# Two of the four block sums of a quad by accumulating DMAs, with the operands in another order

## The chip, the core and the metric

The kernel runs on one core of a Trainium2 chip. The metric is the device time of one execution in microseconds (us); the time before is the median of three runs. Engines are named as in the profile: PE is TensorE (matmuls), PEld its weight load, DVE VectorE, ACT ScalarE, POOL GpSimd, and SP SyncE, which here only issues DMAs. Each engine works through its own queue of instructions in order and waits on semaphores for the others.

## The reference

One decoder block on 256 tokens of width 2048, all in float32: a mixer (gated linear attention beside a short gated convolution, merged by two sigmoid gates) and a SwiGLU network, each behind an RMSNorm and with a residual, and a last RMSNorm.

```python
h = h + hybrid_mixer(rmsnorm(h, mix_norm_w[l]), w_in[l], ...)
h = h + swiglu(rmsnorm(h, ffn_norm_w[l]), w_gate_up[l], w_down[l])
return rmsnorm(h, final_norm_w)

proj = jnp.einsum('bsd,de->bse', h, w_in)          # 2048 -> 16400 columns
(q, k, v, g_out, gk_low, gate_b, gate_c, xc, merge_a, merge_b) = jnp.split(proj, SPLIT_IDX, axis=-1)
y_a = (o * silu(g_out)); y_b = gate_b * causal_depthwise_conv(gate_c * xc, conv_w)
merged = sigmoid(merge_a) * y_a + sigmoid(merge_b) * y_b
out = jnp.einsum('bse,ed->bsd', merged, w_out)

gu = jnp.einsum('bsd,df->bsf', h, w_gate_up)       # 2048 -> 2 x 5632
gate, up = jnp.split(gu, [FFN_HIDDEN], axis=-1)
out = jnp.einsum('bsf,fd->bsd', silu(gate) * up, w_down)
```

Nearly all of the work is in the four weight matrices: `w_in`, `w_out`, `w_gate_up` and `w_down`.

## The kernel before

**Pieces.** Every weight matrix is cut into pieces of 128 partitions x 1024 float32 (512 KB), which the host lays out so that one DMA brings one piece. `stream_list` is the order in which the pieces are used, from the first k, q, v columns through the gates and the output projection to the hidden layer and the down projection.

**Split in two.** A float32 product is made of three matmuls in the fp32r type (`mm3`, lines 347 to 349): each operand is split into a high part and a rest. For a weight piece, ACT casts the raw tile to `hi` (line 238) and DVE subtracts to get `lo` (line 243). There are five raw tiles (`wraw`), six `hi` and five `lo`. `load_piece` issues a piece's DMA (line 232 or 295, on SP) and its cast, and `finish_low` the subtraction one piece later; `take` keeps this at most five pieces ahead of PE (`LOOK`).

**Plain pieces.** Most groups of 512 columns are worked through piece by piece (`eights`, `down`): two rows of blocks times two halves of the tokens, twelve matmuls for a piece.

**Quads with seven products.** Twelve pairs of groups, four in the gates (`gc0`/`xc0` to `gc3`/`xc3`) and eight of the hidden layer's (`fg`/`fu` 0, 3 to 7, 9 and 10), are computed with seven block products instead of eight, a form of Strassen's method (`sevens`). For each of four quads q of such a pair there are four blocks of weights, two of the first key and two of the second. The seven products of a quad are called 11, t1, t3, t2, t4, 21 and 22, six matmuls each. 11, 21 and 22 take a loaded block as it is. t1 to t4 take sums of blocks, made by `sum_of`: tile `y` holds block 11, tile `x` the second key's first block; t1 is y + x, written to a raw tile (line 259); then x grows in place by a third block (t3), by y (t2) and by a fourth block (t4), each time by a DVE addition (line 265). The third and the fourth block are loaded into raw tiles first. Between two of these additions x must have been cast and subtracted, so `sum_of` calls `finish_low` ahead of the next.

**The order.** `seven_list` names the products of a pair: for each quad 11, t1, t3, t2, t4, and at the end the 21 and 22. `mixed` deals the plain pieces that run beside a pair out among them, one behind each sum (with more than 16 of them a second round begins with the 21 and 22). `FIRST` places the first hidden pair by hand among the plain pieces of the output projection. What the code records is put on each engine's queue by a scheduling layer that may move instructions, except those that are pinned (`pin`).

**Round it.** POOL issues the copies and loads of the convolution (`conv`, lines 886 to 894) and three loads of h (line 1007). The gates' results are merged on DVE (lines 907 and 908, pinned) and transposed on PE (`transpose_block`, line 595). A group's PSUM bank comes free when DVE or ACT has taken its result, for the down projection the addition on line 1098; the plain groups have three banks in turn (`lent`).

Of the kernel before, what the change touches and what calls it, by code (L numbers as in the profile page):

```python
# [8 lines left out]
F32 = mybir.dt.float32  # L9
# [3 lines left out]
ALU = mybir.AluOpType  # L13
AX = mybir.AxisListType

P = 128
# [3 lines left out]
KC = D // P  # L20
# [60 lines left out]

FIRST = {0: (6, 6, 8, 10, 12), 1: (14, 14, 16, 18, 20), 2: (22, 22, 23, 24, 26), 3: (28, 28, 29, 30, 31)}
FIRST_END = (31, 32)
SEVENS = ((3, 16), (4, 15), (5, 16), (6, 15), (7, 16), (9, 15), (10, 15))
PLAIN = (1, 2, (0, (0, 1, 2)), (1, (3, 4, 5)), 8, (2, (6, 7, 8)))

# [8 lines left out]
    return first + [p for g in out[3:] for p in g]  # L97


def seven_list(pair):  # L100

    out = [(what, q) for q in range(4) for what in ("11", "t1", "t3", "t2", "t4")]
    twos = (("21", 0), ("21", 1), ("22", 0), ("21", 2), ("22", 1), ("21", 3), ("22", 2), ("22", 3))
    return [(pair, e) for e in out + list(twos)]


def mixed(pair, eights, early=False):

    if pair is None:
        return eights  # L110
    sevens = seven_list(pair)
    sums = ("t1", "t3", "t2", "t4")
    gaps = [0] * len(sevens)
    rest = len(eights)
    while rest > 0:
        for some in (sums + ("11",) if early else sums, ("21", "22")):
            for n, (_, e) in enumerate(sevens):
                if e[0] in some and rest > 0:
                    gaps[n] += 1
                    rest -= 1  # L120
    out, put = [], 0
    for e, n in zip(sevens, gaps):
        out += [e] + eights[put:put + n]
        put += n
    return out


def gates_list():
    return [e for pair, keys in GATES
            for e in mixed(pair, [(key, k) for key in keys for k in range(0, KC, 2)], keys[0] == "gb2")]  # L130


def block_of(key):
# [9 lines left out]
def hidden_list():  # L143

    plain = []
    for what in PLAIN:
        if isinstance(what, tuple):
            part, fs = what
            plain += [e for n in range(len(DOWN[part])) for f in fs for e in down_of(part, n, f)]
        else:  # L150
            plain += [(f"{name}{what}", k) for name in ("fg", "fu") for k in range(0, KC, 2)]
    plain = [(f"wo{n}", k) for n in range(1, 4) for k in range(0, KC, 2)] + plain

    before = {(what, q): FIRST[q][n] for q in range(4) for n, what in enumerate(("11", "t1", "t3", "t2", "t4"))}
    pair = seven_list(("fg0", "fu0"))
    for n, (_, e) in enumerate(pair[20:]):
        before[e] = FIRST_END[0] + n * (FIRST_END[1] - FIRST_END[0]) // 7
    out, put = [], 0
    for key, e in pair:
        out += plain[put:before[e]] + [(key, e)]  # L160
        put = before[e]
# [23 lines left out]
def block_kernel(ctx, tc, x, xt, cols_in, gkw_in, gku_in, gnw, conv_w, finw, w_in, w_out, w_gu, w_dn, out):  # L185
    nc = tc.nc
    pin = tc.keep_in_program_order
    mats = {"w_in": w_in, "w_out": w_out, "w_gu": w_gu, "w_dn": w_dn}

    const = ctx.enter_context(tc.tile_pool(name="const", bufs=1))  # L190
    wraw = ctx.enter_context(tc.tile_pool(name="wraw", bufs=5))
    whi = ctx.enter_context(tc.tile_pool(name="whi", bufs=6))
    wlo = ctx.enter_context(tc.tile_pool(name="wlo", bufs=5))
    aT = ctx.enter_context(tc.tile_pool(name="aT", bufs=1))
# [26 lines left out]
        rows[mat] = rows.get(mat, 0) + 1  # L221
    ready = {}
    hooks = {}
    count = {"loaded": 0, "used": 0, "tick": 0}
    pending = []
    held = {}
    halfway = []

    def fetch(key, k0, pool=wraw, tag="raw"):
        mat, j, n, w = index[(key, k0)]  # L230
        raw = pool.tile([P, n, w], F32, tag=tag, name=tag, bufs={"x": 2, "y": 1}.get(tag))
        nc.sync.dma_start(raw, mats[mat][j].rearrange("p (k c) -> p k c", c=w))
        return raw

    def high(raw, piece, a=0, b=None):
        hi, n = piece[0], piece[2]
        ks = slice(a, b or n)
        nc.scalar.copy(hi[:, ks, :], raw[:, ks, :])  # L238

    def low(raw, piece, a=0, b=None):  # L240
        hi, lo, n = piece
# [3 lines left out]
    def sum_of(pair, what, q):  # L245

        one, two = pair
        if what == "21":
            return fetch(one, 4 * q + 2)
        if what == "22":  # L250
            return fetch(two, 4 * q + 2)
        if what == "11":
            held["y"] = fetch(one, 4 * q, held["pool"], "y")
            return held["y"]
        y = held["y"]
        if what == "t1":
            held["x"] = fetch(two, 4 * q, held["pool"], "x")
            raw = wraw.tile([P, 2, 512], F32, tag="raw", name="raw")
            nc.vector.tensor_tensor(out=raw, in0=y, in1=held["x"], op=ALU.add)  # L259
# [5 lines left out]
        nc.vector.tensor_tensor(out=x, in0=x, in1=other, op=ALU.add)  # L265
        return x

    def load_piece():


        i = count["loaded"]
        count["loaded"] += 1
        if i < len(stream):
            key, k0 = stream[i]
            if isinstance(k0, tuple):
                n, w = 2, 512
                raw = sum_of(key, *k0)
                step = n
            else:
                mat, j, n, w = index[(key, k0)]  # L280
                raw = wraw.tile([P, n, w], F32, tag="raw", name="raw")

                step = n // 2 if i < 2 else n
            piece = [whi.tile([P, n, w], F32R, tag="hi", name="hi"), None, n]
            if isinstance(k0, tuple):
                high(raw, piece)
                halfway.append((raw, piece, key, k0))
            else:
                if i < 2:
                    piece[1] = wlo.tile([P, n, w], F32R, tag="lo", name="lo")  # L290
                for a in range(0, n, step):
                    b = a + step
                    if (i, a) in hooks:
                        hooks.pop((i, a))()
                    nc.sync.dma_start(
                        raw[:, a:b, :], mats[mat][j, :, a * w:b * w].rearrange("p (k c) -> p k c", c=w))
# [944 lines left out]
```

## Time and profile before

| | |
|---|---|
| three runs | 1506.49, 1505.09, 1506.01 us; median 1506.01 |
| the profiled execution | 1504.81 us, of which the span from the first to the last instruction is 1503.1 |
| granted TensorE clock, mean | 0.999 |
| HBM read | 351.03 MB, 235 GB/s over the span |
| DMA queues' share of 16 engines' span | SP's 70.8%, POOL's 2.2%, ACT's 0.3% |
| casts of x on ACT (line 238) | 144, waiting 207.1 us in total for DVE's sums |
| POOL's longest waits | 353.5 us in four, for the convolution's input |

The stages by time: the attention part to about 203 us, the gates to about 700, output projection and the first hidden pair to about 850, hidden layer and down projection to about 1475, and then the last norm and the stores.

How to read the rows: a group shows line, engine, operation, out<-in with shapes, the count, busy time, mean nanoseconds of one, and the idle time ahead of them with what ended it. A row of the timeline shows the start, the duration, engine and line. A row of the stages shows, behind its two bounds, the length and then each engine's busy time, TensorE's clock, the DMA engines' busy share and the rate. A row of the DMA issues ends with the size of one and the median time from issue to landing.

### The profile page before, as it was taken

The numbers are of one execution on the slowest core, as the hardware profiler recorded it, in microseconds if no ns is written. First come the engines' busy times: TensorE is split into PE (matmuls) and PEld (weight loads), VectorE is DVE, ScalarE is ACT, GpSimd is POOL, SyncE is SP. The second block draws the span as 40 slices with busy tenths as digits, with TensorE's granted clock in tenths as the row PEclk, the third lists the DMA queues.
The fourth block names the chain that finished last, engine by engine and source line by source line (L and its number), as shares of the span: only waits on it lengthen the run. The fifth ranks groups of instructions, "written<-read, shape, count | busy, mean of one in ns | idle before, by whom it ended". The sixth has DMA issues, their size and how long they took to land.

```text
span 1503.1 us, 19370 instructions
## 1 busy us (share of the span) xinstructions
PE 1489.7 (99%) x7064; PEld 1244.8 (83%) x7064; DVE 1277.8 (85%) x1283; ACT 864.1 (57%) x977; POOL 38.0 (3%) x60
## 2 busy tenths in 40 slices
PE   9999999999999999999999999999999999999997
PEld 8989988888887888888888888888888788888887
DVE  6785868979979878966689999999999999999975
ACT  7773546655655655654566755655565556565553
POOL 0030000000000000000000000000000000000000
PEclk9999999999999999999999999999999999999999
DMA  9656557876876878787677777776877788787782
GB/s 349 201 172 174 177 166 251 288 225 234 285 259 232 297 237 257 249 258 215 209 221 219 238 253 251 250 253 218 275 242 239 259 255 277 242 264 234 231 297 90
DMA packets 100128, 358.58 MB, mean 239 GB/s; under 512 B 11492, under 2 KB 11620, under 8 KB 99904
## 3 DMA queue, kind: packets, MB, share of 16 engines
q1 hardware_dynamic: 96656, 346.73, 70.8%
q0 software_dynamic: 2800, 8.89, 2.2%
q10 hardware_dynamic: 576, 1.72, 0.3%
q8 instruction: 55, 0.90, 0.2%
q14 instruction: 41, 0.34, 0.1%
HBM read 351.03 MB, written 2.10 MB: 235 GB/s over the span
## 4 chain that ended last, share of the span: by engine, by line
PE 53%; DVE 1%; issue 0%; ACT 0%; DVEq 0%; ACTq 0%
PE fg L347 8%; PE fg L349 8%; PE fg L348 8%; PE dn L347 5%; PE dn L349 5%; PE dn L348 5%; PE wo L347 2%; PE wo L348 2%; PE wo L349 2%; PE fu L349 1%; PE fu L347 1%; PE fu L348 1%; PE trb L595 1%; PE mb L349 0%; PE mb L348 0%
## 5 line engine op out<-in xcount | busy, mean ns | idle before, releaser
L243 DVE TENSOR_TENSOR lo<-raw,hi 128x1024 fp32r<-128x1024 f32 (+1 forms) x506 | 612.0, 1217 | 110.9 <-ACT hi L238 27.9
L238 ACT CAST hi<-raw 128x1024 fp32r<-128x1024 f32 (+1 forms) x506 | 523.9, 1047 | 269.9 <-PE gb L349 27.7
L238 ACT CAST hi<-x 128x1024 fp32r<-128x1024 f32 x144 | 151.7, 1053 | 267.4 <-DVE x L265 207.1
L243 DVE TENSOR_TENSOR lo<-x,hi 128x1024 fp32r<-128x1024 f32 x144 | 176.1, 1223 | 37.5 <-ACT hi L238 26.6
L347 PE MATMUL dn<-lo,acth 128*128 128x512 f32 (+1 forms) x368 | 140.7, 382 | 1.7 <-DVE h L1098 0.9
L349 PE MATMUL dn<-hi,acth 128*128 128x512 f32 (+1 forms) x368 | 139.9, 380 | 0.0
L348 PE MATMUL dn<-hi,actl 128*128 128x512 f32 (+1 forms) x368 | 139.9, 380 | 0.0
L265 DVE TENSOR_TENSOR x<-x,raw 128x1024 f32<-128x1024 f32 x96 | 117.0, 1218 | 12.0 <-DMA raw<-in_w_in_dram 7.7
L347 PE MATMUL fg<-lo,hh 128*128 128x512 f32 x288 | 112.4, 390 | 0.0
L349 PE MATMUL fg<-hi,hh 128*128 128x512 f32 x288 | 112.2, 390 | 0.0
L348 PE MATMUL fg<-hi,hl 128*128 128x512 f32 x288 | 112.2, 389 | 0.0
L347 PE MATMUL fg<-lo,sh 128*128 128x512 f32 x256 | 101.0, 395 | 0.0
L348 PE MATMUL fg<-hi,sl 128*128 128x512 f32 x256 | 99.9, 390 | 0.0
L349 PE MATMUL fg<-hi,sh 128*128 128x512 f32 x256 | 99.8, 390 | 0.0
L347 PEld LDWEIGHTS dn<-lo,acth 128*128 128x128 f32 x368 | 69.2, 188 | 15.8 <-DVE h L1098 1.8
L349 PEld LDWEIGHTS dn<-hi,acth 128*128 128x128 f32 x368 | 69.2, 188 | 13.3
L348 PEld LDWEIGHTS dn<-hi,actl 128*128 128x128 f32 x368 | 69.2, 188 | 12.9
L347 PEld LDWEIGHTS fg<-lo,hh 128*128 128x128 f32 x288 | 54.1, 188 | 11.8 <-DVE lo L243 0.5
L349 PEld LDWEIGHTS fg<-hi,hh 128*128 128x128 f32 x288 | 54.1, 188 | 11.3
L348 PEld LDWEIGHTS fg<-hi,hl 128*128 128x128 f32 x288 | 54.1, 188 | 11.0
L243 DVE TENSOR_TENSOR lo<-y,hi 128x1024 fp32r<-128x1024 f32 x48 | 58.5, 1218 | 4.8 <-ACT hi L238 2.1
L259 DVE TENSOR_TENSOR raw<-y,x 128x1024 f32<-128x1024 f32 x48 | 58.5, 1219 | 4.2 <-DMA y<-in_w_in_dram 3.3
(247 smaller groups left out, 3070.1 us busy)
## 6 DMA issues: line engine op xcount, KB each, us to landing
raw<-in_w_in_dram SPq DMA_DIRECT2D x254, 512.0 KB, 4.5
raw<-in_w_gu_dram SPq DMA_DIRECT2D x176, 512.0 KB, 4.4
raw<-in_w_dn_dram SPq DMA_DIRECT2D x88, 512.0 KB, 4.5
x<-in_w_gu_dram SPq DMA_DIRECT2D x32, 512.0 KB, 4.8
y<-in_w_gu_dram SPq DMA_DIRECT2D x32, 512.0 KB, 3.9
raw<-in_w_out_dram SPq DMA_DIRECT2D x32, 512.0 KB, 4.3
y<-in_w_in_dram SPq DMA_DIRECT2D x16, 512.0 KB, 4.4
x<-in_w_in_dram SPq DMA_DIRECT2D x16, 512.0 KB, 4.8
```

The lines of the kernel that those rows point to most:

```text
L238: nc.scalar.copy(hi[:, ks, :], raw[:, ks, :])
L243: nc.vector.tensor_tensor(out=lo[:, ks, :], in0=raw[:, ks, :], in1=hi[:, ks, :].bitcast(F32), op=ALU.subtract)
L259: nc.vector.tensor_tensor(out=raw, in0=y, in1=held["x"], op=ALU.add)
L265: nc.vector.tensor_tensor(out=x, in0=x, in1=other, op=ALU.add)
L347: nc.tensor.matmul(ps, lhsT=sh, rhs=ml, start=first, stop=False, skip_group_check=onto)
L348: nc.tensor.matmul(ps, lhsT=sl, rhs=mh, start=False, stop=False, skip_group_check=onto)
L349: nc.tensor.matmul(ps, lhsT=sh, rhs=mh, start=False, stop=last, skip_group_check=onto)
L595: nc.tensor.transpose(out=ps[:, j, :], in_=src[:, j * P:(j + 1) * P], identity=ident)
```

## The change

In a quad t3 and t4 are no longer summed by DVE. When t1's sum is recorded, POOL issues a DMA that adds the third block from HBM onto `x` in place (`add_piece`, accumulating); when t2's rest has been recorded, another one adds the fourth block. DVE keeps t1 and t2. The casts of t3 and t4 on ACT are pinned. The raw tiles of the third and fourth block fall away. There are now two `y` tiles: one is the old one, the other takes the place of the fifth raw tile, and the plain raw tiles have four in turn once the first pair has begun.

The order of the products changes: 11, t1, then t4 of the quad before, t3, t2; the last t4 stands among the products at the end (21 four times, 22 twice, t4, 22 twice). `mixed` now deals at least 16 plain pieces, or three quarters of them, to the quads: of four in a quad, three go behind t1 and one behind t3; the rest are spread over the nine at the end. `FIRST` is now a first position and, for each quad, the numbers of plain pieces behind t1, t4, t3 and t2. The `early` case is gone.

```diff
-FIRST = {0: (6, 6, 8, 10, 12), 1: (14, 14, 16, 18, 20), 2: (22, 22, 23, 24, 26), 3: (28, 28, 29, 30, 31)}
-FIRST_END = (31, 32)
+FIRST = (6, ((0, 3, 1, 4), (0, 3, 1, 4), (0, 3, 1, 2), (0, 3, 1, 0)), (1, 0, 0, 1, 0, 0, 0, 0, 0))
...
+def seven_list(pair, gaps):
+    out = []
+    for q in range(4):
+        ahead, fourth, third, second = gaps[q]
+        out += [("11", q, 0), ("t1", q, ahead)]
+        if q:
+            out += [("t4", q - 1, fourth)]
+        else:
+            out[-1] = ("t1", q, ahead + fourth)
+        out += [("t3", q, third), ("t2", q, second)]
+    twos = [("21", 0), ("21", 1), ("21", 2), ("21", 3), ("22", 0), ("22", 1), ("t4", 3), ("22", 2), ("22", 3)]
+    out += [(what, q, n) for (what, q), n in zip(twos, gaps[4])]
+    return [(pair, (what, q), n) for what, q, n in out]
...
+    n = len(eights)
+    quads = max(min(n, 16), n * 3 // 4)
+    gaps = []
+    for q in range(4):
+        c = (quads + 3 - q) // 4
+        places = [0] * 4
+        for i in (0, 0, 0, 2, 3, 1, 0, 2, 3, 1)[:c]:
+            places[i] += 1
+        gaps.append(places)
+    rest = n - quads
+    gaps.append([(i + 1) * rest // 9 - i * rest // 9 for i in range(9)])
...
-    wraw = ctx.enter_context(tc.tile_pool(name="wraw", bufs=5))
+    wraw = ctx.enter_context(tc.tile_pool(name="wraw", bufs=1))
...
+    def raw_tile(n, w):
+        count["raw"] += 1
+        return wraw.tile([P, n, w], F32, tag=f"raw{count['raw'] % count['raws']}", name="raw")
+
+    def first_tile():
+        count["y"] += 1
+        count["raws"] = 4
+        if count["y"] % 2:
+            return wraw.tile([P, 2, 512], F32, tag="raw4", name="y")
+        return held["pool"].tile([P, 2, 512], F32, tag="y", name="y")
...
         if what == "t1":
-            held["x"] = fetch(two, 4 * q, held["pool"], "x")
-            raw = wraw.tile([P, 2, 512], F32, tag="raw", name="raw")
-            nc.vector.tensor_tensor(out=raw, in0=y, in1=held["x"], op=ALU.add)
+            x = held["x", q] = held["pool"].tile([P, 2, 512], F32, tag="x", name="x", bufs=2)
+            fetch(two, 4 * q, x)
+            raw = raw_tile(2, 512)
+            nc.vector.tensor_tensor(out=raw, in0=held["y", q], in1=x, op=ALU.add)
+            add_piece(x, two, 4 * q + 2)
             return raw
-        x = held["x"]
-        if halfway and halfway[-1][0] is x:
-            finish_low()
-        other = y if what == "t2" else fetch(two if what == "t3" else one, 4 * q + 2)
-        nc.vector.tensor_tensor(out=x, in0=x, in1=other, op=ALU.add)
+        x = held["x", q]
+        if what == "t2":
+            if halfway and halfway[-1][0] is x:
+                finish_low()
+            nc.vector.tensor_tensor(out=x, in0=x, in1=held["y", q], op=ALU.add)
         return x
+
+    def add_piece(x, key, k0):
+        mat, j, _, w = index[(key, k0)]
+        nc.gpsimd.dma_start(x, mats[mat][j].rearrange("p (k c) -> p k c", c=w), accum_op=ALU.add)
...
-                high(raw, piece)
+                ins = high(raw, piece)
+                if k0[0] in ("t3", "t4"):
+                    pin(ins)
...
         ready[(key, k0)] = piece
+        if isinstance(k0, tuple) and k0[0] == "t2":
+            add_piece(raw, key[0], 4 * k0[1] + 2)
```

DVE's queue in the pair `fg3`/`fu3`, about one quad, before (line 259 is t1's sum, 265 the sums on x, 243 the subtractions; the numbers behind the names tell tiles apart):

```order
L243 TENSOR_TENSOR lo_7508<-y_7484,hi_7486 128x1024
L243 TENSOR_TENSOR lo_7520<-raw_7504,hi_7506 128x1024
L265 TENSOR_TENSOR x_7502<-x_7502,raw_7534 128x1024
L243 TENSOR_TENSOR lo_7539<-raw_7516,hi_7517 128x1024
L243 TENSOR_TENSOR lo_7551<-x_7502,hi_7537 128x1024
L265 TENSOR_TENSOR x_7502<-x_7502,y_7484 128x1024
L243 TENSOR_TENSOR lo_7568<-raw_7547,hi_7548 128x1024
L243 TENSOR_TENSOR lo_7580<-x_7502,hi_7566 128x1024
L243 TENSOR_TENSOR lo_7593<-raw_7576,hi_7577 128x1024
L265 TENSOR_TENSOR x_7502<-x_7502,raw_7588 128x1024
```

The same place on DVE now (the lines have moved: 281 is t1's sum, 288 the sum on x, 265 the subtractions, 630 a transposed block):

```order
L281 TENSOR_TENSOR raw_7446<-y_7425,x_7444 128x1024
L630 TENSOR_TENSOR actl_7381<-trb_7418,acth_7380 128x4x128
L265 TENSOR_TENSOR lo_7429<-x_7304,hi_7402 128x1024
L265 TENSOR_TENSOR lo_7451<-y_7425,hi_7427 128x1024
L265 TENSOR_TENSOR lo_7469<-raw_7446,hi_7449 128x1024
L265 TENSOR_TENSOR lo_7481<-raw_7465,hi_7466 128x1024
L265 TENSOR_TENSOR lo_7499<-raw_7477,hi_7478 128x1024
L265 TENSOR_TENSOR lo_7509<-raw_7495,hi_7496 128x1024
L265 TENSOR_TENSOR lo_7519<-x_7304,hi_7507 128x1024
L265 TENSOR_TENSOR lo_7531<-x_7444,hi_7517 128x1024
L288 TENSOR_TENSOR x_7444<-x_7444,y_7425 128x1024
L265 TENSOR_TENSOR lo_7548<-raw_7527,hi_7528 128x1024
```

Two of three sums on x are gone. x_7304 is the quad before: lo_7429 is its t2, behind which POOL adds the fourth block, and lo_7519 its t4; lo_7531 is t3 of the new quad, whose third block POOL adds behind the sum raw_7446. Three plain subtractions stand between.

POOL's queue in the gates, from the first convolution's copies to the second's preparation, before (887 and 888 clear the edges):

```order
L893 DMA u1_3112<-u_2826 1x16x32
L894 DMA u2_3113<-u_2826 2x512
L886 DMA taps_3963<-in_conv_w_dram 128x3x512
L888 MEMSET u2_3962 2x512
L887 MEMSET u1_3961 1x512
```

The same stretch of POOL's queue now (294 is the accumulating DMA; 918, 919 and 920 were 886, 887 and 888):

```order
L925 DMA u1_3096<-u_2889 1x16x32
L926 DMA u2_3097<-u_2889 2x512
L294 DMA x_3049<-in_w_in_dram 128x1024
L918 DMA taps_3931<-in_conv_w_dram 128x3x512
L294 DMA x_3215<-in_w_in_dram 128x1024
L294 DMA x_3373<-in_w_in_dram 128x1024
L920 MEMSET u2_3930 2x512
L919 MEMSET u1_3929 1x512
L294 DMA x_3530<-in_w_in_dram 128x1024
```

Four accumulating DMAs of the pair `gc1`/`xc1` now stand between the convolution's rows, in one queue with them.

More of the change, by code (lines that the diff above doesn't have):

```diff
@@ L152, in hidden_list @@
     plain = [(f"wo{n}", k) for n in range(1, 4) for k in range(0, KC, 2)] + plain
[L154 to L161, printed above, removed]
+    put, quads, end = FIRST
+    out = plain[:put]
+    for key, e, m in seven_list(("fg0", "fu0"), [(a, b, c, d) for a, b, c, d in quads] + [end]):
+        out += [(key, e)] + plain[put:put + m]
+        put += m
     plain = plain[put:]
@@ L237, in high @@
         ks = slice(a, b or n)
-        nc.scalar.copy(hi[:, ks, :], raw[:, ks, :])
+        return nc.scalar.copy(hi[:, ks, :], raw[:, ks, :])
     def low(raw, piece, a=0, b=None):
```

40 lines of the change are left out of this document (13 added, 27 removed).

## The prediction

> **What bounds the kernel now.** I read the page's shares first, then the busy times by stage, then PE's waits, then the instructions round two of them.
>
> ```profile
> PE 1489.7 (99%) x7064; PEld 1244.8 (83%) x7064; DVE 1277.8 (85%) x1283; ACT 864.1 (57%) x977; POOL 38.0 (3%) x60
> ```
>
> ```profile
> core 0: us, PE busy (x) PEld busy (x) DVE busy (x) ACT busy (x) POOL busy (x), PEclk, DMA share, GB/s
> 0.00:250.00 250.00, 248.50 (x1492) 220.96 (x1493) 180.37 (x232) 150.39 (x199) 17.66 (x24) 1.00 0.66 210
> 250.00:700.00 450.00, 447.56 (x1980) 368.46 (x1979) 380.08 (x348) 253.76 (x263) 18.07 (x33) 1.00 0.79 255
> 700.00:850.00 150.00, 149.92 (x678) 122.70 (x677) 123.67 (x124) 88.64 (x110) 2.23 (x3) 1.00 0.69 217
> 850.00:1420.00 570.00, 568.76 (x2543) 469.33 (x2542) 536.40 (x508) 329.49 (x348) 0.00 (x0) 1.00 0.77 250
> 1420.00:1475.00 55.00, 54.55 (x244) 44.62 (x244) 43.62 (x47) 33.39 (x39) 0.00 (x0) 1.00 0.77 258
> ```
>
> From 250 to 1475 us, where the change is at work, PE is busy for 447.56 + 149.92 + 568.76 + 54.55 = 1220.8 of 1225.0 us, at full clock. The engine behind it is DVE: 536.40 of 570 us, 94%, in the long stage. So PE is the bound, and all that a lighter DVE can return is PE's idle 4.2 us and what hangs on it. PE's waits in that stretch name it:
>
> ```profile
> engine line waited for: us in total, times, longest us
> PE dn L347 <- DVE h L1098: 0.9, 2, 0.5
> PE trb L595 <- DVE sb L908: 0.9, 1, 0.9
> PE dn L347 <- DVE lo L243: 0.8, 1, 0.8
> PE g L347 <- DVE lo L243: 0.7, 1, 0.7
> PE gc L347 <- DVE lo L243: 0.5, 1, 0.5
> PE gb L347 <- DVE ya L919: 0.2, 1, 0.2
> ```
>
> Together 4.0 us in seven waits, all for DVE. A wait costs more than its idle time:
>
> ```profile
> start us, us, engine line op out<-in xcount [idle before <-releaser]
> 607.72 0.39 PE L348 MATMUL g<-hi,xl 128*128 128x512 f32 x1
> 607.95 0.39 PE L349 MATMUL g<-hi,xh 128*128 128x512 f32 x1
> 608.17 0.39 PE L347 MATMUL g<-lo,xh 128*128 128x512 f32 x1
> 609.45 0.66 PE L595 MATMUL trb<-ident,sb 128*128 128x128 f32 x4 [0.89 <-DVE sb L908]
> ```
>
> Matmuls of 0.39 us start every 0.227 us (607.72, 607.95, 608.17), so after an idle 0.89 us the next start is 1.28 late where 0.23 was due: 1.05 lost, 0.16 more than the wait. Seven waits: 4.0 + 7 x 0.16 = **5.1 us**. That is the most that the change can give. Two of them (the `dn` waits for h) look like this on DVE:
>
> ```profile
> 1174.18 1.22 DVE L265 TENSOR_TENSOR x<-x,raw 128x1024 f32<-128x1024 f32 x1
> 1175.32 1.28 DVE L1098 TENSOR_TENSOR h<-dn,h 128x512 f32<-128x512 f32 x2
> ```
>
> A block sum stands in front of the addition that frees PE's bank. The sum is one of those that the change takes away.
>
> **What goes.** The sums are these groups:
>
> ```profile
> L265 DVE TENSOR_TENSOR x<-x,raw 128x1024 f32<-128x1024 f32 x96 | 117.0, 1218 | 12.0 <-DMA raw<-in_w_in_dram 7.7 <-DMA raw<-in_w_gu_dram 3.8
> L265 DVE TENSOR_TENSOR x<-x,y 128x1024 f32<-128x1024 f32 x48 | 58.6, 1221 | 0.7
> L259 DVE TENSOR_TENSOR raw<-y,x 128x1024 f32<-128x1024 f32 x48 | 58.5, 1219 | 4.2 <-DMA y<-in_w_in_dram 3.3 <-DMA y<-in_w_gu_dram 0.7
> ```
>
> The 96 of the first row (t3 and t4 of 12 blocks x 4 quads) become accumulating DMAs; the order confirms it, 144 additions on x before and 48 after. 117.0 us leave DVE, all beside PE's stream, so they are worth nothing by themselves; in the long stage 28 quads lose 56 x 1.22 = 68 us, and DVE falls from 94% to (536.4 - 68.3) / 570 = 82%. What that returns is the waits above. I let six of the seven go and keep the one of `trb` for sb (1.05 us): it hangs on two pinned additions of the merge, which stay. 5.1 - 1.05 = **4.05 us gained**.
>
> **What the DMAs cost.** No accumulating DMA is in this trace. The nearest rows:
>
> ```profile
> raw<-in_w_gu_dram SPq DMA_DIRECT2D x176, 512.0 KB, 4.4
> x<-in_w_gu_dram SPq DMA_DIRECT2D x32, 512.0 KB, 4.8
> u<-u POOLq DMA_DIRECT2D x8, 448.0 KB, 7.7
> taps<-in_conv_w_dram POOLq DMA_DIRECT2D x4, 768.0 KB, 11.3
> h<-in_x_dram POOLq DMA_DIRECT2D x3, 512.0 KB, 7.5
> ```
>
> Landing: not below 4.4 us, a plain load of 512 KB; above, 11.3 us, the slowest large row of POOL's queue. I take 8, next to u<-u (7.7), which also reads SBUF, and to h (7.5), the same size on the same queue.
>
> How late may it be? These rows enter:
>
> ```profile
> L243 DVE TENSOR_TENSOR lo<-x,hi 128x1024 fp32r<-128x1024 f32 x144 | 176.1, 1223 | 37.5 <-ACT hi L238 26.6 <-PE wo L347 4.3 <-PE gb L347 1.3
> L238 ACT CAST hi<-x 128x1024 fp32r<-128x1024 f32 x144 | 151.7, 1053 | 267.4 <-DVE x L265 207.1
> L423 DVE TENSOR_TENSOR v<-fg,v 128x512 f32<-128x512 f32 x8 | 5.5, 687 | 0.1
> 849.51 0.33 SPq L295 DMA_DIRECT2D raw<-in_w_gu_dram  x1
> 332.49 0.61 POOL L889 DMA_DIRECT2D u<-u  x1 [117.83 <-DVE u L954]
> ```
>
> PE gives a product of the quads six matmuls, 6 x 0.227 = 1.36 us, and a plain piece twelve, 2.72 us. A quad runs 11, t1, three plain, t4 of the quad before, t3, one plain, t2. There are five lo buffers, so lo of a piece is written when PE has finished the piece five before it. The accumulation for t4 starts after lo of t2; from then to the earliest time of lo for t4 PE passes a plain piece, t4, t3, a plain one, t2 and 11, 10.9 us; less 1.22 (lo of t2), 0.61 (issue) and 1.05 (hi of t4) this leaves about **7.6 us free**. PE itself lacks the piece only after t1 and three plain more, 9.5 us, less 1.2: **16 us**. For t3 the free time is about 10 us. At 8 us ACT idles for 0.4 us at t4 and PE never; at 4.4 or 11.3 PE doesn't wait either. Cost 0, with ACT's slack (329.49 of 570 us busy) as its cover; past 16 us each further one costs PE 36 us, one for each t4 inside a block (3 x 12).
>
> Behind a late sum stands ACT's whole queue, since its hi is pinned: the next casts, the copies out of PSUM. Behind the DMA on POOL stand in the gates the loads and copies of the convolution. Before, POOL stood idle there, 117.83 us ahead of the first copy; now rows of both are interleaved, and each DMA's releaser on DVE comes in the same order as the rows do, so I price that at 0. Issuing costs POOL little:
>
> ```profile
> 333.08 0.55 POOL L890 DMA_DIRECT2D u<-u  x1
> 332.10 1.28 DVE L919 TENSOR_TENSOR sb<-sb,mb 128x512 f32<-128x512 f32 x2
> 333.29 1.22 DVE L243 TENSOR_TENSOR lo<-raw,hi 128x1024 fp32r<-128x1024 f32 x1
> ```
>
> 0.5 to 0.6 us each, 96 of them some 55 us on a queue with 38.0 us of work, and DVE's 1.22 us is no longer beside it. Sum 0. The Trainium skill speaks against such a DMA (SBUF — State Buffer, Summary: rules for kernel authors): to hide one that POOL issues under a DVE operation, issue it from ACT or SP, since its descriptors are starved while DVE holds the shared port. If each issue waited for one DVE instruction, landing would be 9.2 instead of 8 us and the sum still 0; the two rows above show no such wait, and the page itself ties it to modes of DVE that a tensor_tensor hasn't.
>
> The 16 DMA engines: a block (28 products, 16 plain) is 360 matmuls, 81.6 us, and moves 40 x 0.524 MB, 257 GB/s (row: 250). What they can do shows from 735 to 743 us:
>
> ```profile
> DMA packets 885, 3.22 MB, mean 403 GB/s; under 512 B 98, under 2 KB 98, under 8 KB 884
> ```
>
> Eight of the 40 now accumulate. If one takes an engine as long as a copy, nothing changes; at three times, 56 units are 360 GB/s, still under 403; at four times, 411, and the engines become the bound. I take less than three: 0. The Trainium skill (Collectives: The Full Stack, The bandwidth ceiling: the fold count and why AG ≠ RS ≠ AR) finds a DMA that adds half as fast as one that copies, because it reads two sources: 308 GB/s, the same 0 by its estimate; no row here shows it.
>
> **What else moves.** The ring of plain raw tiles shrinks from five to four, the fifth alternates with the y tile. In the last nine products of a block, 1.36 us each, the second `22` takes the tile of the second `21`: from there PE needs it after 12.2 us, of which 1.3 (lo), 0.3 (issue), 1.05 (hi), 1.22 (lo) and three closing operations of DVE (3 x 0.69) go: 6.3 us for a landing of 4.4. Cost 0 with 1.9 us to spare; before, the tile came 6.8 us earlier. Plain pieces now stand side by side, so where a group of them ends between two, the next needs a bank that DVE has had 1.4 us less to free. Two such waits of 0.6 were there before; I add 0.4 us. From SP's queue 96 loads go (0.33 us each, on an engine that only waits); where an x or y waits there for its tile, the raw loads behind it wait for casts that stand later in DVE's order anyway: 0.
>
> **Sum.** 4.05 - 0.4 = **3.65 us**. The profiled execution took 1504.81 us (span 1503.1 and 1.7 around), so 1501.2 of its kind; the median of the runs is 1506.01, 1.2 above it, so **1502.4 us**, 0.24% faster. About 0.2%, 3 us, is what a measurement of this kernel can tell from no change.
>
> **Rivals.**
> *Nothing to be had.* PE's stream is the bound, DVE's relief stays hidden, and the new order puts waits of its own where plain pieces meet: some 14 ends of groups; if a third cost 0.6 us, 2.9 us are given back: 1505.3. For it: 99% PE, and waits that come from order as much as from load. Against: six waits with a sum or a lo in front.
> *The ring of four.* In the twos a landing over 6.3 us makes PE wait for the second `22`. At 7.5 us that is 1.2 us in each of the 8 blocks with two or no plain pieces there, 10 us: 1512; at 9.5 us 26: 1528. For it: loads of x take 4.8 us already, and accumulations share the engines. Against: only one accumulation falls into that stretch.
> *The sums land late.* Landing over 16 us, or engine time of four copies. At 18 us, 36 x 2 = 72: 1578. For it: no row bounds it from above. Against: POOL's 448 KB copy takes 7.7.
> *The scheduler undoes it*, sums left on DVE: the order excludes it.
>
> **How the numbers follow.** Forecast 0.52 (1500.5, all seven waits gone and 0.4 not added, to 1504); nothing to be had 0.19; ring of four 0.15; late sums 0.14. The range goes from 1500, half a microsecond under the best, to 1516, which takes in half of the ring's cases and leaves out the late sums. Of the forecast's own cases a tenth falls short of 3 us: faster 0.47; same 0.25; slower 0.28.
>
> **What would show it.** Right: PE's waits for h, lo and ya gone from its list, DVE near 82% from 850 to 1420, x on POOL's queue landing in about 8 us, ACT's waits for that DMA under 1 us each. Wrong: PE waiting for lo in the last products of the blocks (ring), ACT's hi waiting for the DMA x by microseconds with PE behind it (late sums), DMA shares of 1.0 (engines), or new waits of `dn` for h (order).

## The result, and the profile after

The changed kernel takes **1565.51 us** (median of four runs, 1564.02 to 1570.28) where the kernel before takes 1506.11 (four runs beside it): ratio 1.040, 95% interval 1.038 to 1.042. It is 4% slower; the forecast was 1502.4 with a range up to 1516. The profiled execution's span is 1562.9 us, 59.8 more than before.

Busy times by engine, from the page:

```profile
PE 1504.1 (96%) x7064; PEld 1251.5 (80%) x7064; DVE 1177.1 (75%) x1187; ACT 867.5 (56%) x977; POOL 119.3 (8%) x156
```

DVE's busy time fell by 100.7 us (the rows of the sums that left it add up to 117.0), and PE is further from full than before. PE stands idle for 1562.9 - 1504.1 = 58.8 us where it was 13.4 (45 more), and the same 7064 matmuls are busy 14.4 us longer: two losses, 60 us together. The stages of the gates and of the hidden layer (columns as before):

```profile
250.00:700.00 450.00, 438.30 (x1918) 360.65 (x1917) 342.38 (x313) 245.93 (x254) 42.82 (x62) 0.98 0.85 247
850.00:1420.00 570.00, 540.13 (x2369) 440.61 (x2368) 445.00 (x421) 312.96 (x327) 42.12 (x50) 0.98 0.82 235
```

DVE has fallen from 94% to 78%, and PE from 568.76 to 540.13 of 570 us. On average the DMA engines aren't full (0.85 and 0.82), but see the stall below. What PE waits for:

```profile
PE dn L379 <- DVE h L1130: 17.5, 4, 6.2
PE fg L379 <- DVE u L456: 9.3, 5, 3.6
PE gb L379 <- DVE ya L951: 4.4, 1, 4.4
PE trb L627 <- DVE actl L630: 3.9, 4, 1.8
PE ma L379 <- ACT ya L960: 3.7, 1, 3.7
```

Hardly one wait is for a piece. PE waits for PSUM banks: h, u and ya are the instructions that read a bank out and so free it, and in each of the longer waits they stand in DVE's or ACT's queue behind a cast or a subtraction that has itself waited. Those waits are on ACT, first now, then before:

```profile
ACT hi L260 <- DMA x<-in_w_gu_dram: 66.7, 20, 7.9
ACT hi L260 <- DMA raw<-in_w_in_dram: 55.1, 31, 7.9
ACT hi L260 <- DMA raw<-in_w_gu_dram: 20.0, 18, 5.6
ACT hi L260 <- DMA raw<-in_w_dn_dram: 15.7, 20, 4.4
ACT hi L260 <- DMA x<-in_w_in_dram: 10.7, 2, 5.5
```

```profile
ACT hi L238 <- DMA raw<-in_w_in_dram: 19.2, 19, 4.8
ACT hi L238 <- DMA raw<-in_w_dn_dram: 5.0, 5, 3.0
ACT hi L238 <- DMA raw<-in_w_gu_dram: 3.6, 4, 1.9
```

Two kinds: the accumulated x (77.4 us, new), and plain raw tiles (90.8 us, 27.8 before). The DMA queues and issues from 850 to 1420 us:

```profile
q0 software_dynamic: 7142, 26.05, 26.9%
...
raw<-in_w_gu_dram SPq DMA_DIRECT2D x95, 512.0 KB, 4.8
raw<-in_w_dn_dram SPq DMA_DIRECT2D x59, 512.0 KB, 5.3
x<-in_w_gu_dram POOLq DMA_DIRECT2D x50, 512.0 KB, 7.3
```

An accumulating DMA lands in 7.3 us (median of the 50), less than the 8 I took. But the median mixes two kinds. In 13 of the 25 quads POOL issues t4's DMA directly behind the next quad's t3, and there t4's, the second of the two, takes 7.2 to 10.2 us, median 9.5. The two of the stall shown next, t3's and then t4's:

```profile
x<-in_w_gu_dram POOLq DMA_DIRECT2D x1, 512.0 KB, 7.2
x<-in_w_gu_dram POOLq DMA_DIRECT2D x1, 512.0 KB, 10.0
```

**One stall in full.** The timeline of ACT and POOL, then DVE, then PE, from 1085 to 1113 us, and behind it the row of the stretch in which the two DMAs are under way:

```profile
1085.67 2.00 ACT L260 CAST hi<-x 128x1024 fp32r<-128x1024 f32 x2 [5.59 <-DMA x<-in_w_gu_dram]
1090.47 1.06 ACT L260 CAST hi<-x 128x1024 fp32r<-128x1024 f32 x1 [1.86 <-DVE x L288]
1093.37 1.74 POOL L294 DMA_DIRECT2D x<-in_w_gu_dram  x2 [17.12 <-DVE raw L281]
1104.32 1.99 ACT L260 CAST hi<-x 128x1024 fp32r<-128x1024 f32 x2 [6.57 <-DMA x<-in_w_gu_dram]
1105.40 2.36 DVE L265 TENSOR_TENSOR lo<-x,hi 128x1024 fp32r<-128x1024 f32 x2 [5.75 <-ACT hi L260]
1108.94 1.28 DVE L1130 TENSOR_TENSOR h<-dn,h 128x512 f32<-128x512 f32 x2
1104.39 0.39 PE L381 MATMUL dn<-hi,acth 128*128 128x512 f32 x1
1109.68 0.80 PE L379 MATMUL dn<-lo,acth 128*128 128x512 f32 x1 [4.90 <-DVE h L1130]
1110.27 0.63 PE L380 MATMUL dn<-hi,actl 128*128 128x512 f32 x1
1110.70 0.63 PE L381 MATMUL dn<-hi,acth 128*128 128x512 f32 x1
```

```profile
1093.00:1105.00 12.00, 11.78 (x52) 9.41 (x51) 6.65 (x6) 4.63 (x5) 1.68 (x2) 1.00 0.98 249
```

Read it from the top. At 1085.67 ACT casts t4 of one quad and t3 of the next, one behind the other: t4's DMA has just landed, t3's had landed 4.4 us before, but its cast stands behind that of t4. 4.80 us later (two casts, two subtractions, the sum for t2) it casts t2. 2.90 us after that POOL begins to issue t3's and t4's next DMAs, one behind the other (1.74; lo of t2, which t4's waits for, is done meanwhile), and 9.21 us after the second issue ACT can cast again: 4.80 + 2.90 + 1.74 + 9.21 = **18.65 us for one round**. PE needs 5 x 1.36 + 4 x 2.72 = 17.7 us for the quad. ACT's wait ahead of the pair of casts grows in this round from 5.59 to 6.57 us, by about that difference; the larger part of it was there one quad earlier. While ACT waits, DVE waits behind it (5.75 us), and only after that wait comes h at 1108.94, for which PE has stood since 1104.78 (1104.39 + 0.39). Afterwards matmuls start every 0.43 us (1110.27, 1110.70) where 0.227 is usual. Of the seven idle times of over 3 us, six are followed by such starts, 57 of them in all, 0.20 us lost each: the larger part of the 14 us.

Two things in these rows are easily passed over. First, what released POOL at 1093.37 was not lo of t2 but t1's sum (raw, L281), and that sum has a path of its own back to t4: lo of t4 frees the x tile, SP's load of the next x is issued at 1088.00 and lands in 3.6 us, and the sum starts at 1091.61. Its group shows such waits, 12.4 us in all:

```profile
L281 DVE TENSOR_TENSOR raw<-y,x 128x1024 f32<-128x1024 f32 x48 | 58.6, 1221 | 12.8 <-DMA x<-in_w_gu_dram 7.1 <-DMA x<-in_w_in_dram 5.3
```

t4's DMA, behind t3's, is issued at 1094.27, and lo of t2 was done at 1093.97. So the round closes by two arms that are equally long to 0.3 us here. Second, the DMA engines are busy to 0.98 while the two DMAs are under way; in all 13 cases together the median is 0.96.

### The profile page after: what moved, and what is told of

It reads as the page before. It is cut to its first block, busy times and chain, and to the rows that moved or that the text cites. A ratio compares the mean times of both kernels' runs of the same rounds, so it can differ in the third digit from the quotient of the medians.

```text
span 1562.9 us, 19383 instructions
## 1 busy us (share of the span) xinstructions
PE 1504.1 (96%) x7064; PEld 1251.5 (80%) x7064; DVE 1177.1 (75%) x1187; ACT 867.5 (56%) x977; POOL 119.3 (8%) x156
## 5 line engine op out<-in xcount | busy, mean ns | idle before, releaser
L294 POOL DMA_DIRECT2D x<-in_w_gu_dram x64 | 54.1, 850 | 683.5 <-DVE raw L281 257.4
L381 PEld LDWEIGHTS dn<-hi,acth 128*128 128x128 f32 x368 | 70.4, 191 | 13.7
L281 DVE TENSOR_TENSOR raw<-y,x 128x1024 f32<-128x1024 f32 x48 | 58.6, 1221 | 12.8 <-DMA x<-in_w_gu_dram 7.1
L379 PEld LDWEIGHTS fg<-lo,sh 128*128 128x128 f32 x256 | 48.5, 189 | 21.3 <-DVE u L456 11.7
L260 ACT CAST hi<-y 128x1024 fp32r<-128x1024 f32 x48 | 50.4, 1050 | 27.0 <-PE dn L381 11.3
```

What stands on the lines that cost most here:

```text
L260: return nc.scalar.copy(hi[:, ks, :], raw[:, ks, :])
L281: nc.vector.tensor_tensor(out=raw, in0=held["y", q], in1=x, op=ALU.add)
L294: nc.gpsimd.dma_start(x, mats[mat][j].rearrange("p (k c) -> p k c", c=w), accum_op=ALU.add)
L379: nc.tensor.matmul(ps, lhsT=sh, rhs=ml, start=first, stop=False, skip_group_check=onto)
L381: nc.tensor.matmul(ps, lhsT=sh, rhs=mh, start=False, stop=last, skip_group_check=onto)
```

## The experiments

The theories that the runs were to tell apart. **A/L**: the accumulated sums are late, because they form a loop: t4's landing releases its cast, behind which ACT has t3's; t2's sum waits for t3; lo of t2 releases the next t4 (the arm by the load of x was not part of the theory). **B**: the new order costs by itself. **R** (C in e1): four raw tiles are too few. A rival to all: the loss goes by the work that the DMA engines do. The runs of the kernel before that stood beside them have medians of 1505.3 to 1505.7 us. In e1 to e12 the line numbers are those of the changed kernel.

| run | us, median (range) | ratio to before, 95% |
|---|---|---|
| e1, without the 96 DMAs | 1499.61 (1499.15 to 1499.80) | 0.9945 to 0.9975 |
| e2, both copy | 1504.08 (1502.48 to 1508.73) | 0.998 to 1.000 |
| e3, t3's alone | 1508.51 (1504.59 to 1512.84) | 1.001 to 1.003 |
| e4, t4's alone | 1507.04 (1505.99 to 1512.26) | 1.000 to 1.002 |
| e5, t3's copies, t4's adds | 1523.99 (1521.68 to 1527.88) | 1.011 to 1.015 |
| e6, t3 ahead of t4 | 1564.57 (1560.82 to 1565.16) | 1.037 to 1.041 |
| e7, the same, other plain piece | 1550.26 (1546.14 to 1553.21) | 1.028 to 1.032 |
| e8, new order, DVE sums | 1532.36 (1530.11 to 1535.85) | 1.016 to 1.021 |
| e9, five raws | 1543.92 (1540.85 to 1557.68) | 1.022 to 1.031 |
| e10, five raws, DVE sums | 1507.26 (1505.78 to 1509.55) | 0.999 to 1.001 |
| e11, five raws, t3 ahead of t4 | 1522.91 (1520.40 to 1526.17) | 1.009 to 1.013 |
| e12, five raws, one y, DVE sums | 1548.47 (1547.73 to 1557.71) | 1.026 to 1.032 |
| e13, e11's hidden blocks, old gates | 1505.29 (1504.50 to 1508.45) | 0.999 to 1.001 |
| e14, the same, other plain piece | 1509.86 (1505.66 to 1514.77) | 1.002 to 1.004 |
| e15, t4's alone, old gates | 1506.67 (1506.17 to 1508.57) | 1.000 to 1.002 |
| e16, t3's alone, old gates | 1511.81 (1510.84 to 1513.99) | 1.003 to 1.006 |

### The DMAs by dose: e1 to e5

e1 leaves both calls out; every other instruction stands on its engine as in the changed kernel.

```diff
-            add_piece(x, two, 4 * q + 2)
+            pass
...
-            add_piece(raw, key[0], 4 * k0[1] + 2)
+            pass
```

> Leaves out the 96 accumulating DMAs (t3 and t4 are computed from sums that lack a block); every other instruction stands where it stands in the changed kernel, the ring of four raws and the order included. Theory A (sums that land late hold ACT and DVE, and the copies out of PSUM behind them come late): the whole loss goes, 1500 to 1507 us, PE's waits for h, u and ya down to under 5 us together. Theory B (the new order, plain pieces side by side, costs by itself): 1535 us or more, the waits of dn for h stay near 17 us. Theory C (the ring of four raws): 1515 to 1540, and ACT's waits for raw stay near 90 us.

1499.61 us, as theory A has it. Two rows of e1, the page's busy times and the stage from 850 us:

```profile
PE 1487.5 (99%) x7064; PEld 1244.8 (83%) x7064; DVE 1180.9 (79%) x1187; ACT 876.2 (58%) x977; POOL 37.9 (3%) x60
```

```profile
850.00:1420.00 570.00, 568.68 (x2541) 468.76 (x2540) 483.23 (x455) 337.95 (x348) 0.00 (x0) 1.00 0.63 200
```

DVE's relief and the new order are worth 5.9 us against before; B is out for this load, and the 66 us up to the changed kernel come with the 96 DMAs. In e2 they copy:

```diff
-        nc.gpsimd.dma_start(x, mats[mat][j].rearrange("p (k c) -> p k c", c=w), accum_op=ALU.add)
+        nc.gpsimd.dma_start(x, mats[mat][j].rearrange("p (k c) -> p k c", c=w))
```

> The 96 DMAs copy in place of adding (t3 and t4 are computed from the copied block alone); order, queue and waits as in the changed kernel. If what costs is a latency that any transfer of POOL's queue has here (release, issue 0.85 us, some 6 to 7 us to land): 1545 to 1566. If it is the adding, which takes a DMA engine about twice as long: landing near 5 us, 1505 to 1520.

1504.08. POOL's queue as such is not the cost; that the DMA adds is. e3 and e4 leave out one of e1's two calls each.

> Only the 48 accumulations of t3 are left, those of t4 are left out; order as in the changed kernel. By the free times of the prediction (t3 some 10 us, t4 7.6) and theory A: t3 alone lands in 6 to 7 us and costs little, 1502 to 1515 us. If the accumulations as such cost by their number (engine time, POOL): about half of the loss, 1530 to 1540.

> Only the 48 accumulations of t4 are left, those of t3 are left out; order as in the changed kernel. Theory A: t4 is the one with 7.6 us free, so most of the loss that is left stands here, 1515 to 1540; without t3's transfer issued 0.9 us ahead of it it lands in 6 to 7 us, so less than the whole. By number: 1530 to 1540.

1508.51 and 1507.04: either alone costs 7 to 9 us over e1, both together 66. That isn't a cost by number, and e4 is a miss: theory A had put most of the loss on t4 alone. The queues and issues of POOL from 850 to 1420 us, first of e2 (copies), then of e4 (one addition at a time):

```profile
q0 software_dynamic: 7920, 28.84, 15.5%
...
x<-in_w_gu_dram POOLq DMA_DIRECT2D x55, 512.0 KB, 4.8
```

```profile
q0 software_dynamic: 3888, 14.16, 15.4%
...
x<-in_w_gu_dram POOLq DMA_DIRECT2D x27, 512.0 KB, 5.5
```

Half the bytes take the same share of the engines: an accumulation costs an engine twice the time of a copy (28.84/15.5 against 14.16/15.4). The Trainium skill's rule that the prediction cites (Collectives: The Full Stack, The bandwidth ceiling: the fold count and why AG ≠ RS ≠ AR) has the same factor of two. Where t4's are alone they land in 5.5 us, t3's alone in 6.4 (e3), and the second of two issued together in 9.5; in e2, where they copy, the second of two takes 5.0.

e5 lets t3's DMA copy and t4's add:

```diff
-    def add_piece(x, key, k0):
+    def add_piece(x, key, k0, **how):
...
-        nc.gpsimd.dma_start(x, mats[mat][j].rearrange("p (k c) -> p k c", c=w), accum_op=ALU.add)
+        nc.gpsimd.dma_start(x, mats[mat][j].rearrange("p (k c) -> p k c", c=w), **how)
...
-            add_piece(raw, key[0], 4 * k0[1] + 2)
+            add_piece(raw, key[0], 4 * k0[1] + 2, accum_op=ALU.add)
```

> The DMA of t3 copies in place of adding (t3 is computed from the copied block alone), that of t4 adds; nothing else differs from the changed kernel. Theory L (a loop: t4's DMA is released by lo of t2, its cast stands ahead of t3's on ACT, t2's sum waits for t3, and lo of t2 releases the next t4; in the changed kernel one round takes 18.6 us where PE's quad lasts 17.7, so the lag grows): with t3's transfer taking half the engine time the pair lands 1.6 us or more earlier, a round is 15 to 17 us, under 17.7, and the lag heals: 1503 to 1515 us. If instead the loss goes by the engine time of the DMAs (copies of both 4.5 us over the kernel without them, adds of both 66): about halfway, 1525 to 1545.

1523.99, between the two expectations: two copies 4.5 us over e1, copy and addition 24, two additions 66. The cost rises faster than the engines' work, as a lag would that grows once a round is longer than the quad, but it starts earlier than L alone allows. (The second of two takes 7.7 us to land here, which by the sum above makes a round of some 16 us, an estimate.) Something else adds to the lag.

### The order and the ring: e6 to e12

e6 puts t4 of the quad before behind t3, which takes hi and lo of t3 and t2's sum out of t4's round:

```diff
-        out += [("11", q, 0), ("t1", q, ahead)]
+        out += [("11", q, 0), ("t1", q, ahead), ("t3", q, third)]
...
-        out += [("t3", q, third), ("t2", q, second)]
+        out += [("t2", q, second)]
...
-        for i in (0, 0, 0, 2, 3, 1, 0, 2, 3, 1)[:c]:
+        for i in (0, 0, 0, 3, 2, 1, 0, 2, 3, 1)[:c]:
```

> Same work and DMAs as the changed kernel, all of it; t4 of the quad before is put behind t3 instead of ahead of it, and the plain piece from between t3 and t2 to behind t2. Theory L: hi and lo of t3 and t2's sum no longer stand in t4's round, which falls to some 14 us: 1502 to 1515 us, ACT's waits for the DMA x under 25 us in all. If it is the landing of the pair (9 us) as such that holds ACT, whatever the order: 1545 or more.

1564.57: nothing gained, a miss for L. But ACT's waits for x of w_gu fell from 66.7 to 26.5 us, and those for raws of w_gu and w_dn rose from 35.7 to 88.8:

```profile
ACT hi L260 <- DMA raw<-in_w_gu_dram: 47.6, 26, 6.8
ACT hi L260 <- DMA raw<-in_w_dn_dram: 41.2, 25, 5.8
ACT hi L260 <- DMA x<-in_w_gu_dram: 26.5, 12, 5.1
```

One lag had shrunk and another stood in its place. e7 is e6 with the last line of the diff left as it was:

> As e6, but the plain piece stays behind t3, so that t4 and t2 follow it directly. Theory L: the round of t4 is cut as in e6, but x of the next quad is loaded only behind lo of t4, three products (4.1 us) ahead of t1, for which it needs some 8 us: a lag of some 4 us at each t1 that doesn't grow: 1505 to 1530 us.

1550.26, above the expected 1505 to 1530, and better than e6, where I expected it to be worse. e8 keeps the changed kernel's order and tiles and gives the sums back to DVE, with 96 loads more through the raw tiles:

```diff
-            nc.vector.tensor_tensor(out=x, in0=x, in1=held["y", q], op=ALU.add)
+        other = held["y", q] if what == "t2" else fetch(two if what == "t3" else one, 4 * q + 2)
+        nc.vector.tensor_tensor(out=x, in0=x, in1=other, op=ALU.add)
```

> The order, the four raws and the two y of the changed kernel, but t3 and t4 are summed by DVE from a raw tile, as before. If the new order is harmless or better by itself (the kernel without the 96 DMAs took 1499.6): 1500 to 1508 us. If the order needs DVE's relief, or four raws are too few for the 96 loads more on SP's queue: 1512 to 1540.

1532.36. No DMA adds here, and 27 us are lost all the same. This is theory R, or the order. In the changed kernel the ring shows at 957 us (ACT's timeline, then the same place in e9):

```profile
957.46 1.05 ACT L260 CAST hi<-raw 128x1024 fp32r<-128x1024 f32 x1 [0.30 <-PE fg L381]
964.09 1.05 ACT L260 CAST hi<-raw 128x1024 fp32r<-128x1024 f32 x1 [5.57 <-DMA raw<-in_w_gu_dram]
```

```profile
962.49 1.06 ACT L260 CAST hi<-raw 128x1024 fp32r<-128x1024 f32 x1 [1.62 <-PE fu L381]
964.17 1.05 ACT L260 CAST hi<-raw 128x1024 fp32r<-128x1024 f32 x1 [0.62 <-DMA raw<-in_w_gu_dram]
```

Four raws were cast one behind the other, their tiles come free nearly together, and the loads go out as one burst; the DMA rows of 955 to 966 us in the changed kernel give them

```profile
raw<-in_w_gu_dram SPq DMA_DIRECT2D x4, 512.0 KB, 8.1
```

to land, with an accumulation among them. The place is the end of a block, the products 21 and 22. e9 has five raws from the first hidden block on:

```diff
-        count["raws"] = 4
+        count["raws"] = 5 if dpool else 4
         if count["y"] % 2:
-            return wraw.tile([P, 2, 512], F32, tag="raw4", name="y")
+            return (dpool or wraw).tile([P, 2, 512], F32, tag="y2" if dpool else "raw4", name="y")
```

> The changed kernel with five raw tiles in place of four from the first hidden block on (700 us on); the second y tile gets 4 KB of its own there, the bf16 scratch of the sums of squares moves into a tile that is free then. The gates keep the ring of four. Theory R (with four raws, four pieces in a row are loaded, cast and subtracted as one burst, and ACT then stands for a whole landing): most of the loss after 850 us goes (29.9 us of PE idle in 850 to 1420 and the slow matmuls behind it), 1520 to 1535 us, with the gates' loss left. Theory L (the loop by t4): the ring is no part of it, 1555 to 1566.

> e8 (order of the changed kernel, sums by DVE) with the five raws of e9. Theory R: the 27 us that e8 lost against before lie in the hidden blocks and come from 96 loads more through four raws: 1502 to 1510 us. If the new order itself does not carry DVE's sums: 1525 to 1533.

> e6 (t3 ahead of t4) with the five raws of e9. If R is what held e6 (its ACT waited 89 us for raws of w_gu and w_dn, 27 for the accumulated x): 1515 to 1535, and below e9 if L has a part of the loss too. If neither: 1555 or more.

e9 1543.92 (its profiled execution, with a span of 1555.9, is at the upper end of its runs): the ring is worth 22 us, less than R had expected. e10 1507.26: with DVE's sums the ring is 25 of the 27 us that e8 lost, so the order itself carries them. e11 1522.91: with five raws, t3 ahead of t4 gives the 21 us that it did not give with four. The new order also parts the two DMAs: from 850 to 1420 us 4 of them are issued directly behind another, where e9 has 13. So e11 does not tell the shorter round from the parted transfers. e11's stages:

```profile
250.00:700.00 450.00, 435.05 (x1913) 356.82 (x1912) 340.16 (x312) 244.82 (x254) 42.82 (x62) 1.00 0.84 247
850.00:1420.00 570.00, 565.69 (x2527) 465.99 (x2526) 477.29 (x449) 336.97 (x348) 45.46 (x54) 1.00 0.87 251
```

PE is at 565.69 of 570 in the hidden layer again, with all the accumulations at work and the DMA engines busier on average than in any run above (0.87). So the engines' work as such is not the loss. What is left stands in the gates (435.05), which still have four raws.

e12 asked for the order alone, with the tiles of the kernel before in every block:

```diff
-        count["raws"] = 4
-        if count["y"] % 2:
-            return wraw.tile([P, 2, 512], F32, tag="raw4", name="y")
-        return held["pool"].tile([P, 2, 512], F32, tag="y", name="y")
+        one_tile = held["pool"]
+        return one_tile.tile([P, 2, 512], F32, tag="y", name="y")
```

> The order of the changed kernel with sums by DVE and with the tiles of the kernel before in every block, gates too: five raws, one y. From the kernel before it differs by the order alone. Theory R: 1503 to 1512 (one y behind t2's sum may cost a landing of 4.4 us now and then). If the order costs by itself: 1520 or more.

A miss, 1548.47: ACT waited 108.2 us for y. In the new order 11 of the next quad follows t2 directly, so one y tile is loaded only when the sum of t2 is done. The second y, for which the change gave up a raw tile, is needed by its order.

### What is left: e13 to e16

e13 gives the gates the order, the tiles and the DVE sums of the kernel before, and keeps e11's hidden blocks:

```diff
+    def by_dma(what, pair):
+        return what in ("t3", "t4") and pair[0][:2] == "fg"
...
-    return [e for pair, keys in GATES for e in mixed(pair, [(key, k) for key in keys for k in range(0, KC, 2)])]
+    return [e for pair, keys in GATES
+            for e in old_mixed(pair, [(key, k) for key in keys for k in range(0, KC, 2)], keys[0] == "gb2")]
```

> Gates as in the kernel before (its order, five raws, one y, sums by DVE); hidden blocks as in e11 (both DMAs, t3 ahead of t4, five raws, two y). If the 17 us left in e11 lie in the gates: 1503 to 1509 us, PE busy over 446 us from 250 to 700. If the DMAs still cost in the hidden blocks: 1512 or more.

1505.29, as before to 0.1%. Its stages, and its accumulations from 850 to 1420 us:

```profile
250.00:700.00 450.00, 448.66 (x1988) 370.27 (x1987) 378.82 (x347) 253.82 (x262) 18.05 (x33) 1.00 0.80 253
850.00:1420.00 570.00, 565.02 (x2524) 465.79 (x2523) 480.35 (x452) 334.55 (x346) 46.71 (x55) 1.00 0.87 249
```

```profile
x<-in_w_gu_dram POOLq DMA_DIRECT2D x55, 512.0 KB, 7.0
```

They land in 7.0 us, hardly sooner than in the changed kernel. With an order and a ring that leave room for it the same price costs the hidden layer some 4 us of PE's busy time (565.02; e1 568.68, before 568.76), and the kernel as a whole takes as long as before. e14 is e13 with the plain piece of a quad behind t3 in place of behind t2:

> As e13, with the plain piece of a quad behind t3 (as in e7) in place of behind t2. By the loop's account x of the next quad then comes 4 us late at each t1, a lag that does not grow: 1506 to 1520, above e13. If the place doesn't matter: as e13 within 2 us.

1509.86, 4.6 us over e13, within what the loop's account gave. (That e7 came out ahead of e6 with four raws I can only guess at: in e6 a plain piece, t1 and three plain ones stand in a row, five raws on four tiles.) e15 and e16 change `by_dma` to one product and keep t4 ahead of t3:

> As e13, but t3 is summed by DVE from a raw tile again, and t4 (by DMA) stands ahead of t3 as in the changed kernel. A single DMA lands in 5.5 us, and the round by t3 is gone: 1501 to 1506. DVE carries 32 sums more than in e13. If the order ahead of t3 costs: 1510 or more.

> As e15, but t3 by DMA and t4 summed by DVE. t3's DMA is released by the sum of t1, no round: 1501 to 1507, within 3 us of e15.

1506.67 and 1511.81: both above their expectation or at its end, e16 by 5 us. Why t3 alone costs more than t4 alone wasn't followed up; its DMA also lands later, in 6.0 us against 5.6 (e3 and e4: 6.4 and 5.5). No version that computes the whole beats the kernel before.

## Why the prediction was wrong

**What bounds the kernel, and what DVE's relief returns: right in size.** PE's stream, with at most 5.1 us to be had and 4.05 forecast; e1 gained 5.9, though it moves 50 MB less as well. DVE itself is relieved less than forecast: in the long stage by 53 us in e1 (536.40 to 483.23), where the prediction takes off 68.

**The landing of a DMA: right in the median, wrong where it counts.** 8 us taken, 7.3 measured in the long stage; but t4's, for which the margin was worked out, takes 9.5 us where it is issued directly behind a t3. The prediction prices each DMA as if it were alone. Its engine time, taken at under three copies, is two: right, and the engines still come to 0.98 for the length of such a landing, which a mean over the block (0.82) does not show.

**POOL's issue: small, but off.** 0.5 to 0.6 us taken, 0.84 measured (42.12 us for 50); a copy takes 0.53 (29.22 us for 55 in e2). It adds to the round.

**"Cost 0, with ACT's slack (329.49 of 570 us busy) as its cover; past 16 us each further one costs PE 36 us": this step failed.** The 7.6 us free for t4 (the terms given, 10.9 less 1.22, 0.61 and 1.05, leave 8.0) were counted from a lo of t2 that is on time. But that lo depends, by t2's sum, on t3's cast, and that stands on ACT behind the cast of the t4 before; the load of the next x hangs on that t4 as well. So the lag of one quad is handed on to the next, and the question isn't whether 8 us fit into 7.6 once but whether a whole round fits into a quad: 18.65 against 17.7. ACT's slack is no cover where ACT waits at the head of its own queue. And the 16 us were a limit for PE's want of the piece, where PE in truth wants the banks. The prediction names what stands behind a late sum, "ACT's whole queue ... the copies out of PSUM", and prices it at 0; in the trace the reads of PSUM on DVE and ACT (h, u and ya) are 35 of the 59 us that PE stands idle.

**Late sums as a rival: the outcome, not the condition.** The rival's 1578 us are near the 1565.5 measured, but it asked for landings over 16 us or the engine time of four copies. The longest landing of the 96 took 13.7 us and the engine time is that of two copies, so that its number comes near is luck. Its sign did appear, ACT's hi waiting for the DMA x by microseconds with PE behind it, and so did the order's, new waits of `dn` for h, although e1 shows that the order is not their cause.

**The ring of four, "Cost 0 with 1.9 us to spare": failed too, and the rival had the place.** The 6.3 us allowed for a landing of 4.4; where a ring is refilled as a burst beside an accumulation it measured 8.1, and by the rival's own sum (1.2 us for each of 8 blocks at 7.5) that is 14 us. e9 shows 22. The burst is where the rival put it, in the last products of a block, but its sign, PE waiting for lo there, did not appear: PE waits for u behind it. So the size is right in part by luck.

**The two were not independent.** t3 ahead of t4 gives nothing with four raws and 21 us with five. From the changed kernel down: five raws in the hidden blocks 21.6, t3 ahead of t4 21.0, old gates 17.6 us, and 1505.3 is reached.

**Order, 0.4 us for banks where plain pieces meet: right in kind.** In e1 these meetings cost nothing that shows. With DVE late by 5 us they are where the lag comes to PE.

What the runs show and what they don't: that the DMAs, the ring and the order of t3 and t4 each carry their part is shown by taking each away. That the lag goes round the loop as described is read from the rounds (18.65 in the changed kernel; in e9, with five raws, casts at 1083.67 and 1102.96, 19.3) and fits e11; e11 also moved a plain piece and parted the two DMAs, so it is not proved by one edit. Nor is it told apart how much of the loss is the round and how much the late landing of the second DMA. In the gates I did not separate the ring from the pairs: with four raws, one DMA alone (e3, e4) leaves PE at 449.90 of 450 us there and both together at 438.30; with four raws and DVE's sums (e10) it is 444.71, with 447.56 before, so the ring by itself accounts for the smaller part. The convolution's rows between the DMAs on POOL's queue, priced at 0, were not tried apart. Whether the pin on the casts matters wasn't tried.

## What to carry to other kernels

Before an engine's work is handed to a transfer, follow the release of that transfer back until it closes on itself, and compare the round with the time that the bottleneck takes for the same unit of work: a delay that fits once may still grow by a microsecond at each turn. Price a wait by what is queued behind the waiting instruction on its engine, not by who needs its result; here it was the reads of PSUM. Price two transfers that are issued together as two. And a tile taken from a ring is priced at the worst burst with the other traffic of the new kernel, not at the median landing of the old.

## What the hardware showed

An accumulating DMA of 512 KB keeps the engines busy twice as long as a copy, lands in 5.5 to 6.4 us where only one of t3 and t4 is used (copy: 4.8) and in 9.5 as the second of two issued together (copy: 5.0), and costs POOL 0.84 instead of 0.53 us to issue.

A PE that idled for over 3 us mostly came back slow: after 4.90 us its matmuls started every 0.43 instead of 0.227 us until 1113.26, 3.6 us later, and the granted clock from 1107 to 1113 us was 0.50; after idle times of up to 2 us there was little or none of that, and after one of 3.27 us none. The Trainium skill (TensorE: Matmul & The Clock Gate, Part 1) has this as a clock that falls to a half after an idle window of about 3.4 us and gives a start every 426.7 ns at 512 columns while it is cold. The trace agrees with the spacing (0.43) and with the half, but less so with the length: 3.11 us were enough here, 2.60 in e9 (clock 0.50 from 296.5 to 299.8), and 3.27 once were not. The prediction had priced a wait at its length and 0.16 us; beyond 3 us it was in six of seven cases a wait and some 2 us (1.5 to 2.9).
